# Weight sums by accumulating transfers in a seven-product feed-forward block (one core of Trainium2)

## The chip, the cores and the metric

The kernel runs on one core of one Trainium2 chip. Its time is device time in microseconds (us) of one launch; lower is better. Shown for the kernel before are three runs and one profiled execution.

## The reference

The reference is an encoder trunk of two layers on 512 positions of width 1024, in float32. Each layer is a half-step feed-forward block, a token mixer, and another feed-forward block, each with a residual and a layer norm. The change touches only the feed-forward blocks:

```python
def swiglu(x, w_gate, w_up, w_down):
    return (jax.nn.silu(x @ w_gate) * (x @ w_up)) @ w_down
```

`w_gate` and `w_up` are 1024 x 2816, `w_down` is 2816 x 1024. The block's result is halved, added to the scaled input, and normalised.

## The kernel before, in words

Every matrix product is made as three products of rounded parts: `split` (L90) makes of a float32 tile a rounded half (`hi`, tag `whi` for weights, ScalarE, L92) and a remainder (`lo`, tag `wlo`, VectorE, L94), and `mm3` (L124) issues hi*hi, hi*lo and lo*hi to the tensor engine (L127 to L129). A weight tile is fetched by SyncE's queue into a `raw` buffer (`fetch`, L104) and then split (`halves`, L112). There are four `raw` buffers and five each of `whi` and `wlo`; a buffer is taken again when its last reader is done.

Three of the four feed-forward blocks run as `ffn7` (L324), three times in the program. The 22 blocks of 128 hidden columns are made two at a time (a group) by `up` (L341), 11 groups. The first nine groups' share of the product with `w_down` is computed by a scheme with seven products in place of eight: the hidden columns of a pair, the two halves of the positions and the two halves of the output columns form a 2 x 2 by 2 x 2 block product. The activations' seven combinations are made in `up` (L378 to L381, tile `hb`, split into `sl`). After every third group, `down` (L394) does the weights' part for the three groups, nine times in the whole program. It works in two units: a long one of two groups (tiles of 128 x 1024, 512 KB) and a short one of one group (128 x 512, 256 KB). A unit's four weight blocks are w11 and w12 (own buffers `b11`, `b12`, two each, one for each unit) and w21 and w22 (`raw` buffers).

In a unit the first four products need p2, the split of w21; p1, the split of w11; q4, the split of a sum of all four blocks; and q5, the split of t1 = w11 + w12 (a `raw` buffer too). The sums are made in place, by VectorE:

```python
tt(out=t1, in0=w11, in1=w12, op=ALU.add)     # L417
tt(out=w12, in0=w12, in1=w22, op=ALU.add)    # L418
tt(out=w11, in0=w11, in1=w12, op=ALU.add)    # L419
tt(out=w21, in0=w21, in1=w11, op=ALU.add)    # L420
```

PE then takes p2, q4, p1, q5 of the long unit (12 matmuls each), p2, q4, p1, q5 of the short one (6 each), and after them the summed w11, w22 (fetched again) and the summed w12 of both units. PE's order is as written; the order of the instructions on the other engines, and of the loads on SyncE's queue, is set by a scheduler when the program is built, and each engine runs its own in that order. The next group's gate weights are fetched into the `raw` buffers that the short unit leaves. GpSimd has, in these blocks, only the small steps of the layer norm (L145, L146, L180), behind the last groups.

Of the kernel before, what the change touches and what calls it, by code (L numbers as in the profile page):

```python
# [14 lines left out]
ALU = mybir.AluOpType  # L15
# [34 lines left out]
class Trunk:  # L50
# [273 lines left out]
    def ffn7(self, xt, wg, wu, wd, g_ap, b_ap, out=None, fetch=None, groups=(3, 3, 3), res=4):  # L324
# [3 lines left out]
        nc, tc = self.nc, self.tc  # L328
        tt = nc.vector.tensor_tensor
# [4 lines left out]
        with tc.tile_pool(name="act", bufs=1, reuse_waits="tile") as ap, \  # L334
# [50 lines left out]
            def part(b, banks, js, w, start, stop, onto=False):  # L385

                hi, lo = w
                for i, j in enumerate(js):
                    for t in range(2):
                        c = slice(t * P, t * P + P)  # L390
                        self.mm3(banks[t], slots[j][:, 0, b, c], slots[j][:, 1, b, c], hi[:, i], lo[:, i],
                                 start and i == 0, stop and i == len(js) - 1, onto)

            def down(gi):  # L394

                js = list(range(first[gi], first[gi + 1]))
                units = [js[i:i + 2] for i in range(0, len(js), 2)]
                Y, Z, X, V = ([self.bank() for _ in range(2)] for _ in range(4))  # L400

                def take(banks, half, col, scale):
                    for t in range(2):
                        self.add_to(xt[2 * half + t][:, col * 512:col * 512 + 512], banks[t], scale)
                held = []
                for u in units:
                    shape, rows = [len(u), 512], slice(u[0], u[-1] + 1)
                    at_end = u is units[0], u is units[-1]
                    w11, w12 = (ap.tile([P] + shape, F32, tag=n, name=n, bufs=2) for n in ("b11", "b12"))
                    w21 = self.fetch(b21[:, rows], shape)  # L410
                    p2 = self.halves(w21, shape)
                    nc.sync.dma_start(w11, b11[:, rows])
                    p1 = self.halves(w11, shape)
                    nc.sync.dma_start(w12, b12[:, rows])
                    w22 = self.fetch(b22[:, rows], shape)
                    t1 = self.w.tile([P] + shape, F32, tag="raw", name="raw", bufs=RAW)
                    tt(out=t1, in0=w11, in1=w12, op=ALU.add)  # L417
                    tt(out=w12, in0=w12, in1=w22, op=ALU.add)  # L418
                    tt(out=w11, in0=w11, in1=w12, op=ALU.add)  # L419
                    tt(out=w21, in0=w21, in1=w11, op=ALU.add)  # L420
                    q4 = self.halves(w21, shape)
                    q5 = self.halves(t1, shape)
                    part(1, Y, u, p2, *at_end)
                    part(2, Z, u, q4, *at_end)
                    part(0, X, u, p1, *at_end)
                    part(3, V, u, q5, *at_end)
                    held.append((u, shape, rows, w11, w12))
                take(Y, 0, 0, 0.5)
                take(Z, 1, 0, 0.5)
                take(X, 0, 0, 0.5)  # L430
                take(V, 1, 1, 0.5)
                for u, shape, rows, w11, w12 in held:
                    part(4, X, u, self.halves(w11, shape), False, u is units[-1], True)
                take(X, 0, 1, -0.5)
                for u, shape, rows, w11, w12 in held:
                    part(6, V, u, self.load(b22[:, rows], shape), False, u is units[-1], True)
                take(V, 0, 1, 0.5)
                for u, shape, rows, w11, w12 in held:
                    part(5, X, u, self.halves(w12, shape), False, u is units[-1], True)
                take(X, 1, 1, -0.5)  # L440
                take(X, 1, 0, 0.5)

            with self.as_written(mybir.EngineType.PE):
                for fg in range(NF // 2):
                    up(fg)
                    if fg == 0 and fetch is not None:
                        xt = fetch()
                    if fg + 1 in first:
                        down(first.index(fg + 1) - 1)
# [19 lines left out]
            g, b = self.ln_params(g_ap, b_ap, ap)  # L469
# [939 lines left out]
```

## Time and profile before

| | |
|---|---|
| median of three runs | 1802.85 us (1802.31 to 1803.46) |
| profiled execution, its own time | 1803.46 us |
| span of the profile | 1801.7 us |
| PE, DVE, ACT, POOL busy | 1782.3, 1103.5, 709.2, 34.8 us |
| transfers | 213.57 MB, mean 119 GB/s |

Engines: PE is the tensor engine, DVE VectorE, ACT ScalarE, POOL GpSimd, SP SyncE; "q" behind a name means its instruction queue, where transfers are issued. A row of the instruction timeline gives its start and length in us, the engine, the source line, the operation, the tiles written and read, their form, and in brackets how long the engine had been idle before and what it waited for. A row of transfer issues gives the tile and its source, the number, the size of one and the median time from issue to landing.

### The profile page before, as it was taken

Reading aid. Unit: us, or ns where it says so; the run is one execution under the profiler, and the core shown is the slowest. Engines: PE = TensorE matmul, PEld = TensorE weight load, DVE = VectorE, ACT = ScalarE, POOL = GpSimd, SP = SyncE. Lnnn points to the kernel's source line nnn. Section 1 sums busy time; section 2 is a strip of 40 time slices with the busy share of each in tenths; the row PEclk is TensorE's granted clock in tenths of the full one; section 3 lists DMA queues with packets and bytes.
Section 4 is the critical chain, followed back from the end, with each engine's and each line's share of the span. In section 5 each row is a group of like instructions: output and inputs, shape, how many; then the busy total and the mean of one; then the engine's idle time right before and its main releaser. Section 6 shows DMA issues by size and latency. Waiting matters only on the chain.

```text
span 1801.7 us, 22457 instructions
## 1 busy us (share of the span) xinstructions
PE 1782.3 (99%) x8754; PEld 1494.7 (83%) x8754; DVE 1103.5 (61%) x1812; ACT 709.2 (39%) x1019; POOL 34.8 (2%) x119
## 2 busy tenths in 40 slices
PE   9999999999999999999999999999999999999998
PEld 8888888898887888888889888888888898888886
DVE  7956432276766657474746575757488566566664
ACT  4233421255776443333334333333354343333341
POOL 0000000010000100000000000000020000000000
PEclk9999999999999999999999999999999999999999
DMA  6345633255413544243243251514323251515131
GB/s 211 107 125 172 204 100 101 94 172 161 138 62 98 179 167 155 73 134 94 78 151 106 76 163 59 158 59 123 117 88 95 70 182 60 162 62 162 48 127 47
DMA packets 169338, 213.57 MB, mean 119 GB/s; under 512 B 8208, under 2 KB 128784, under 8 KB 169232
## 3 DMA queue, kind: packets, MB, share of 16 engines
q1 hardware_dynamic: 169232, 212.14, 37.5%
q8 instruction: 68, 1.11, 0.3%
q14 instruction: 38, 0.31, 0.1%
HBM read 196.91 MB, written 14.16 MB: 117 GB/s over the span
## 4 chain that ended last, share of the span: by engine, by line
issue 59%; PE 35%; DVE 3%; POOL 1%; ACT 1%; DMA 1%; POOLq 0%; DVEq 0%; ACTq 0%
PE ps L127 11%; PE ps L128 11%; PE ps L129 11%; PE ps L851 1%; POOL rs L146 1%; DVE wlo L94 0%; PE ps L901 0%; PE ps L136 0%; PE ps L893 0%; DVE pl L94 0%; POOL st L180 0%; DMA s5tl<-side 0%; POOL rs L145 0%; DMA raw<-in_wg_dram 0%; PE ps L892 0%
## 5 line engine op out<-in xcount | busy, mean ns | idle before, releaser
L127 PE MATMUL ps<-xh,whi 128*128 128x512 f32 (+1 forms) x1696 | 637.5, 376 | 1.4 <-ACT xh L92 1.4
L128 PE MATMUL ps<-xl,whi 128*128 128x512 f32 (+1 forms) x1696 | 633.3, 373 | 1.7 <-DVE xl L94 1.7
L129 PE MATMUL ps<-xh,wlo 128*128 128x512 f32 (+1 forms) x1696 | 632.9, 373 | 0.0
L94 DVE TENSOR_TENSOR wlo<-raw,whi 128x1024 fp32r<-128x1024 f32 (+1 forms) x325 | 376.0, 1162 | 396.7 <-ACT whi L92 396.1
L92 ACT ACTIVATE whi<-raw 128x1024 fp32r<-128x1024 f32 (+1 forms) x325 | 328.4, 1012 | 604.5 <-PE ps L128 383.1
L127 PEld LDWEIGHTS ps<-xh,whi 128*128 128x128 f32 x1696 | 319.4, 188 | 60.4 <-issue 3.1
L128 PEld LDWEIGHTS ps<-xl,whi 128*128 128x128 f32 x1696 | 319.5, 188 | 56.9 <-DVE xl L94 2.4
L129 PEld LDWEIGHTS ps<-xh,wlo 128*128 128x128 f32 x1696 | 319.4, 188 | 56.4
L127 PE MATMUL ps<-whi,sl 128*128 128x512 f32 x426 | 165.7, 389 | 0.0
L128 PE MATMUL ps<-wlo,sl 128*128 128x512 f32 x426 | 165.7, 389 | 0.0
L129 PE MATMUL ps<-whi,sl 128*128 128x512 f32 x426 | 165.4, 389 | 0.0
L165 DVE SCALAR_TENSOR_TENSOR xb<-ps,xb 128x512 f32<-128x512 f32 x176 | 113.9, 687 | 38.9 <-PE ps L129 38.6
L129 PEld LDWEIGHTS ps<-whi,sl 128*128 128x128 f32 x426 | 80.0, 188 | 16.7
L128 PEld LDWEIGHTS ps<-wlo,sl 128*128 128x128 f32 x426 | 80.0, 188 | 16.6
L127 PEld LDWEIGHTS ps<-whi,sl 128*128 128x128 f32 x426 | 80.0, 188 | 16.6
L368 ACT ACTIVATE th<-ps 128x512 f32<-128x512 f32 x66 | 38.8, 593 | 110.5 <-PE ps L129 110.4
L374 DVE TENSOR_TENSOR hb<-th,ps 128x512 f32<-128x512 f32 x54 | 36.7, 688 | 64.8 <-PE ps L129 64.8
L94 DVE TENSOR_TENSOR sl<-hb,sl 128x1792 fp32r<-128x1792 f32 x27 | 54.6, 2023 | 31.9 <-ACT sl L92 31.9
L92 ACT ACTIVATE whi<-b 128x1024 fp32r<-128x1024 f32 (+1 forms) x54 | 45.8, 849 | 66.9 <-PE ps L129 64.8
L92 ACT ACTIVATE sl<-hb 128x1792 fp32r<-128x1792 f32 x27 | 45.9, 1700 | 44.7 <-DVE hb L381 44.7
L94 DVE TENSOR_TENSOR wlo<-b,whi 128x1024 fp32r<-128x1024 f32 (+1 forms) x54 | 50.7, 952 | 6.1 <-ACT whi L92 6.1
L127 PE MATMUL ps<-whi,xh 128*128 128x256 f32 (+1 forms) x160 | 49.9, 312 | 0.3 <-ACT xh L92 0.3
(339 smaller groups left out, 1953.6 us busy)
## 6 DMA issues: line engine op xcount, KB each, us to landing
raw<-in_wg_dram SPq DMA_DIRECT2D x88, 512.0 KB, 4.4
raw<-in_wu_dram SPq DMA_DIRECT2D x88, 512.0 KB, 3.9
raw<-in_wd_dram SPq DMA_DIRECT2D x61, 512.0 KB, 3.3
raw<-in_ab_in_dram SPq DMA_DIRECT2D x20, 512.0 KB, 4.3
b<-in_wd_dram SPq DMA_DIRECT2D x18, 512.0 KB, 5.1
raw<-in_wd_dram SPq DMA_DIRECT2D x27, 256.0 KB, 2.6
raw<-in_cd_in_dram SPq DMA_DIRECT2D x12, 512.0 KB, 3.6
b<-in_wd_dram SPq DMA_DIRECT2D x18, 256.0 KB, 5.3
```

Of the source, the lines that this page charges most:

```text
L92: nc.scalar.activation(out=hi, in_=src, func=AF.Copy, scale=scale)
L94: nc.vector.tensor_tensor(out=lo, in0=src, in1=hi.bitcast(F32), op=ALU.subtract)
L127: mm(ps, ah, bh, start=start, stop=False)
L128: mm(ps, ah, bl, start=False, stop=False)
L129: mm(ps, al, bh, start=False, stop=stop)
L146: nc.gpsimd.tensor_tensor(out=v[:, 1:2], in0=v[:, 0:1], in1=self.cst[:, 0:1], op=ALU.pow)
L165: self.nc.vector.scalar_tensor_tensor(out=zz, in0=p, scalar=scale, in1=zz, op0=ALU.mult, op1=ALU.add, **({} if total is None else {"accum_ ...
L368: nc.scalar.activation(out=th, in_=bk[0, f], func=AF.Silu)
L374: tt(out=hb[:, 0::7] if f == 0 else hb[:, 1:3], in0=th.rearrange("p (a c) -> p a c", a=2), in1=bk[1, f].rearrange("p (a c) -> p a c", a=2) ...
L851: nc.tensor.matmul(banks[h][:, o:o + w], a[r, i * P:i * P + P], b[r, :w], start=n == 0, stop=n == 2)
```

## The change

The last three of a unit's four adds are replaced by transfers that add the source buffer to what the destination buffer holds. They are issued by GpSimd. t1 stays on VectorE.

```diff
                     tt(out=t1, in0=w11, in1=w12, op=ALU.add)
-                    tt(out=w12, in0=w12, in1=w22, op=ALU.add)
-                    tt(out=w11, in0=w11, in1=w12, op=ALU.add)
-                    tt(out=w21, in0=w21, in1=w11, op=ALU.add)
+                    for a, b in ((w12, w22), (w11, w12), (w21, w11)):
+                        nc.gpsimd.dma_start(a, b, accum_op=ALU.add)
                     q4 = self.halves(w21, shape)
                     q5 = self.halves(t1, shape)
```

PE's and SyncE's instructions keep their order. Lines behind L418 have a number that is one lower after the change. DVE around the first `down`, before; of the long unit b11_6169 is w11, raw_6171 w21, raw_6185 t1, of the short one b11_6246 is w11, b12_6247 w12, raw_6248 w21, raw_6260 w22 and raw_6262 t1:

```order
L94 TENSOR_TENSOR wlo_6179<-b11_6169,whi_6178 128x1024
L419 TENSOR_TENSOR b11_6169<-b11_6169,b12_6170 128x1024
L420 TENSOR_TENSOR raw_6171<-raw_6171,b11_6169 128x1024
L94 TENSOR_TENSOR wlo_6191<-raw_6171,whi_6190 128x1024
L417 TENSOR_TENSOR raw_6262<-b11_6246,b12_6247 128x512
L418 TENSOR_TENSOR b12_6247<-b12_6247,raw_6260 128x512
L94 TENSOR_TENSOR wlo_6195<-raw_6185,whi_6194 128x1024
L374 TENSOR_TENSOR hb_6147<-th_6148,ps_6085 128x2x256
```

The same place after the change, on to the short unit's q4 (wlo_6268) and q5 (wlo_6272):

```order
L94 TENSOR_TENSOR wlo_6179<-b11_6169,whi_6178 128x1024
L94 TENSOR_TENSOR wlo_6191<-raw_6171,whi_6190 128x1024
L94 TENSOR_TENSOR wlo_6195<-raw_6185,whi_6194 128x1024
L417 TENSOR_TENSOR raw_6262<-b11_6246,b12_6247 128x512
L374 TENSOR_TENSOR hb_6147<-th_6148,ps_6085 128x2x256
L374 TENSOR_TENSOR hb_6147<-th_6151,ps_6086 128x512
L379 TENSOR_TENSOR hb_6147<-hb_6147 128x256
L378 TENSOR_TENSOR hb_6147<-hb_6147 128x256
L94 TENSOR_TENSOR wlo_6251<-raw_6248,whi_6250 128x512
L380 TENSOR_TENSOR hb_6147<-hb_6147 128x256
L381 TENSOR_TENSOR hb_6147<-hb_6147 128x256
L94 TENSOR_TENSOR wlo_6256<-b11_6246,whi_6255 128x512
```

The adds are gone, and the short unit's t1 stands behind the remainder of the long q5, where it stood ahead of it. The remainders of q4 (wlo_6191) and, in the short unit, of p1 (wlo_6256) keep their places in the row.

GpSimd after the change, from the last layer-norm step ahead of the first `ffn7` to the second `down`'s first transfers (b12_6170 is w12 and raw_6183 w22 of the long unit):

```order
L146 TENSOR_TENSOR rs_5608<-rs_5608,cst_63 128x1
L419 DMA b12_6170<-raw_6183 128x1024
L419 DMA b11_6169<-b12_6170 128x1024
L419 DMA raw_6171<-b11_6169 128x1024
L419 DMA b12_6247<-raw_6260 128x512
L419 DMA b11_6246<-b12_6247 128x512
L419 DMA raw_6248<-b11_6246 128x512
L419 DMA b12_6820<-raw_6833 128x1024
```

Before, the next layer-norm step of GpSimd (L180) followed here; now 18 transfers of a block stand ahead of it, six for each `down`.

## Rows read from the trace of the kernel before

**Rows 1.** The page: busy time by engine, and one costly group of PE.
```profile
PE 1782.3 (99%) x8754; PEld 1494.7 (83%) x8754; DVE 1103.5 (61%) x1812; ACT 709.2 (39%) x1019; POOL 34.8 (2%) x119
...
L128 PE MATMUL ps<-xl,whi 128*128 128x512 f32 (+1 forms) x1696 | 633.3, 373 | 1.7 <-DVE xl L94 1.7
```

**Rows 2.** Busy us by stretch: length, PE, PEld, DVE, ACT, POOL, clock, DMA share, GB/s.
```profile
648.50:684.50 36.00, 36.00 (x161) 29.80 (x160) 19.88 (x21) 10.17 (x12) 0.00 (x0) 1.00 0.19 61
684.50:713.20 28.70, 28.70 (x128) 23.79 (x127) 24.75 (x35) 13.47 (x15) 0.00 (x0) 1.00 0.46 142
...
872.10:900.80 28.70, 28.70 (x128) 23.76 (x127) 24.76 (x35) 13.48 (x15) 0.00 (x0) 1.00 0.33 94
```

**Rows 3.** Two of the adds by line: ns min/median/max, first and last start, forms.
```profile
L418 DVE TENSOR_TENSOR b<-b,raw x18: 692/959/1227, 655.5 to 1691.8; 128x1024 f32<-128x1024 f32 x9, 128x512 f32<-128x512 f32 x9
...
L420 DVE TENSOR_TENSOR raw<-raw,b x18: 691/960/1227, 672.5 to 1704.5; 128x1024 f32<-128x1024 f32 x9, 128x512 f32<-128x512 f32 x9
```

**Rows 4.** Timeline of DVE around the first `down`.
```profile
669.95 1.22 DVE L94 TENSOR_TENSOR wlo<-b,whi 128x1024 fp32r<-128x1024 f32 x1
...
674.88 1.22 DVE L94 TENSOR_TENSOR wlo<-raw,whi 128x1024 fp32r<-128x1024 f32 x1 [1.19 <-ACT whi L92]
676.14 0.69 DVE L417 TENSOR_TENSOR raw<-b,b 128x512 f32<-128x512 f32 x1
...
683.97 1.37 DVE L374 TENSOR_TENSOR hb<-th,ps 128x512 f32<-128x512 f32 x2 [2.67 <-PE ps L129]
...
688.08 0.69 DVE L94 TENSOR_TENSOR wlo<-b,whi 128x512 fp32r<-128x512 f32 x1 [0.68 <-ACT whi L92]
...
689.53 0.69 DVE L420 TENSOR_TENSOR raw<-raw,b 128x512 f32<-128x512 f32 x1
```

**Rows 5.** Timeline of ACT around the first `down`.
```profile
673.79 1.06 ACT L92 ACTIVATE whi<-raw 128x1024 fp32r<-128x1024 f32 x1
...
687.96 1.69 ACT L92 ACTIVATE sl<-hb 128x1792 fp32r<-128x1792 f32 x1
690.35 0.63 ACT L92 ACTIVATE whi<-raw 128x512 fp32r<-128x512 f32 x1 [0.70 <-DVE raw L420]
...
705.05 1.06 ACT L92 ACTIVATE whi<-raw 128x1024 fp32r<-128x1024 f32 x1 [0.72 <-PE ps L129]
```

**Rows 6.** Timeline of PE in the first `down`.
```profile
687.40 0.39 PE L128 MATMUL ps<-wlo,sl 128*128 128x512 f32 x1
...
695.56 0.39 PE L128 MATMUL ps<-wlo,sl 128*128 128x512 f32 x1
...
696.92 0.39 PE L128 MATMUL ps<-wlo,sl 128*128 128x512 f32 x1
```

**Rows 7.** Transfer issues: count, size of one, median us to landing.
```profile
raw<-in_wg_dram SPq DMA_DIRECT2D x88, 512.0 KB, 4.4
...
raw<-in_wd_dram SPq DMA_DIRECT2D x61, 512.0 KB, 3.3
...
raw<-in_wd_dram SPq DMA_DIRECT2D x27, 256.0 KB, 2.6
...
x<-in_x_dram SPq DMA_DIRECT2D x6, 512.0 KB, 6.8
...
x<-in_x_dram SPq DMA_DIRECT2D x4, 256.0 KB, 5.5
...
side<-side SPq DMA_DIRECT2D x32, 32.0 KB, 2.0
```

**Rows 8.** Timeline of SP's queue around the first `down`.
```profile
677.59 4.07 SPq L106 DMA_DIRECT2D raw<-in_wd_dram  x2
692.79 1.78 SPq L106 DMA_DIRECT2D raw<-in_wg_dram  x2
```

**Rows 9.** GpSimd: a group by line, and its first step behind the first `ffn7`'s `down`s.
```profile
L145 POOL TENSOR_SCALAR rs<-mv 128x1 f32<-128x1 f32 x4 | 3.7, 928 | 22.2 <-DVE mv L1234 17.0 <-DVE pm L1264 5.2
...
952.65 0.19 POOL L180 TENSOR_TENSOR st<-st 128x1 f32<-128x1 f32 x1 [330.77 <-ACT ps L176]
```

## The prediction

> **What bounds the kernel now.** I read the page first, then busy time by stretches, then the order of events around one of the changed adds. The page's busy times [rows 1] have the tensor engine (PE) at 1782.3 of 1801.7 us, so whatever is not PE's own work costs time only where it makes PE wait. The stretches [rows 2] show this at the changed place: in the last 36 us before a `down` and in the 28.7 us of the `down` itself PE is busy 36.00 of 36.00 and 28.70 of 28.70 us, at a granted clock of 1.00 (its 2.4 GHz level). DVE has 16 us free in the first stretch and 4 in the second. All nine `down`s read alike (the first and, of the third, the `down` itself are shown), so what one costs is taken nine times.
>
> Next, when PE needs what. In the first `down`, which PE begins at about 684.5 with the long unit's p2, the first product with the long q4's remainder starts at 687.40, the one with the short p2's remainder at 695.56, with the short q4's at 696.92 [rows 6]; each rounded half is wanted 0.23 us sooner. ACT takes the summed long w21 at 673.79 [rows 5]; the sum of the short one ends on DVE at 689.53 + 0.69 = 690.22 [rows 4]. So the long q4 has 13.6 us from its sum to PE, the short one 6.7, of which the split itself takes some. **The short unit is the tight place.**
>
> **What is removed.** Three adds in each of 18 units, 54 in all, at medians of 959 and 960 ns for two of them [rows 3] and the third like them: 54 x 0.96 = 51.8 us of DVE. It is worth nothing: PE does not wait for DVE here [rows 2]. In the whole run PE's idle time is 1801.7 - 1782.3 = 19.4 us, and none of it lies in these stretches.
>
> **What is added.** 54 transfers on chip, 27 of 512 KB and 27 of 256 KB, each waiting for the one before. Call L the time of a long one from the end of its wait to landing, S that of a short one. The first (w12 += w22) has no bearing in the long unit: its inputs are ready when the pair sum t1 is (DVE starts the first add that it replaces at 655.5 [rows 3]), 15 us before the second is allowed.
>
> The second (w11 += w12) overwrites w11, so it waits for the remainder of p1, which DVE ends at 669.95 + 1.22 = 671.17 [rows 4]. The third lands at 671.17 + 2L. ACT then rounds (1.06 us [rows 5]) and DVE subtracts (1.22 us): with 0.1 us of hand-over the long q4 is ready at 673.5 + 2L. PE asks for it at 687.40: **no stall in the long unit up to L = 6.9 us**.
>
> But DVE and ACT work in order, and the late q4 holds up what stands behind it. DVE can begin q4's remainder at 671.17 + 2L + 1.13 = 672.30 + 2L. Behind it come q5's remainder, t1 of the short unit, the five steps of the third activation group and two short remainders, the last of them p1's: 1.26 + 1.26 + 0.73 + 4.12 = 7.37 us by the starts and lengths in [rows 4] (674.88 to 676.14 for a long remainder; 0.69 and 0.04 to the next for the short t1; 683.97 to 688.77 less 0.68 us of idle time for the rest). So the short p1 remainder ends at 679.67 + 2L if that is later than now, 688.08 + 0.69 = 688.77: up to L = 4.55 nothing moves. Call this time E. The first short transfer starts after the short t1, at 675.55 + 2L, and lands S later; if that is later than E, it takes E's place.
>
> From E the second and third short transfers take 2S, then ACT 0.63 and DVE 0.69 us with 0.15 of hand-over [rows 4, 5]. PE asks at 696.92. **Stall per `down` = E + 2S - 695.44.** With E as now, S may be 3.33 us; with L above 4.55 the stall is 2(L + S) - 15.77, so L + S may be 7.9 us.
>
> **The price of L and S.** No transfer in the profile is issued by GpSimd, none accumulates, and the only ones between buffers on chip are of 32 KB, 2.0 us [rows 7]. From below: plain loads of the same weights, landing after 3.3 us (512 KB) and 2.6 us (256 KB), medians. From above: the slowest plain loads of these sizes, x's, at 6.8 and 5.5 us [rows 7]. An accumulating transfer must read both operands. The two plain medians give 0.7 us for 256 KB over 1.9 us that do not depend on size; charging the bytes twice gives 1.9 + 2.8 = 4.7 and 1.9 + 1.4 = 3.3 us. GpSimd's issue comes on top: its one-column operations take 0.19 to 0.93 us [rows 9], and I take the upper end, 0.9, since making a transfer's list is more work than one column. So **L = 5.6, S = 4.2**, nearer to the plain loads because the transfer queues are quiet here (share 0.19 and 0.46 in [rows 2]). The upper bounds get the second reading too: 6.8 + 1.4 = 8.2 and 5.5 + 0.7 = 6.2.
>
> The Trainium skill, "DMA: Bandwidth & Descriptors", section "Rules for kernel authors", says that an accumulating transfer reads its destination and writes it later; no run here shows it yet. With that alone and no price for the issue, 4.7 and 3.3, an estimate, the stall would be 2 x 8.0 - 15.77 = 0.2 us per `down`, some 2 us in all.
>
> **The sum.** E: 679.67 + 11.2 = 690.87, against 675.55 + 11.2 + 4.2 = 690.95 for the first short transfer; the later counts. Stall 690.95 + 8.4 - 695.44 = 3.9 us, nine times 35 us. Against the profiled execution's own 1803.46 us that is 1838.7; the median of the three runs stands 0.6 lower, so **1838 us**, 2.0% slower.
>
> **What else moves, at no price.** SP's order of loads is the same, but its waits are not. The short b22 load, second of the pair begun at 677.59, now waits for the first short transfer, some 9 us later; behind it the next group's gate weights, issued at 692.79 [rows 8], wait for the short q4 split, to about 701. They land after 4.4 us [rows 7], at 705; ACT wants the first at 705.05 now [rows 5] and 3.9 us later then, and PE not before the `down` ends at 713.2. If that cover goes, the next group starts late by the shortfall. The third activation group reaches PE's short unit (remainder needed at 695.56 [rows 6]) through DVE and ACT behind the late q4: 672.30 + 2L + 6.7 for its last step, 1.69 for its rounding [rows 5] and 1.22 x 1.75 = 2.1 for its remainder of 1792 columns by the 1024 of [rows 4], so 694.0 at L = 5.6; it becomes a stall of its own from L = 6.4. On GpSimd the 18 transfers of a feed-forward block stand ahead of its layer-norm steps; the first of these runs at 952.65 [rows 9], 52 us after the last `down` of that block ends at about 901, so it is covered.
>
> **Rivals.**
> *Hidden.* An accumulating transfer costs what a plain load of its size does: L + S = 3.3 + 2.6 = 5.9, under 7.9, and S under 3.33. No stall, 1803 us, not slower. For it: the slack is real and the queues are quiet. Against it: the bytes are read twice, and a software engine issues. It decides as long as L + S stays under 7.9 and S under 3.33. Chance 0.18. The Trainium skill, same page, section "Anatomy of one DMA — SWDGE (gpsimd) path", speaks for this one: it fits a GpSimd transfer as 2.0 us plus its bytes at 436 GB/s, an estimate of 3.2 and 2.6 us, so no stall and 1803 us. The plain loads of [rows 7] agree with it, but SP issued those.
>
> *Dear.* The transfers are slow themselves: L = 8.2, S = 6.2. Then E = 675.55 + 16.4 + 6.2 = 698.15, the stall 698.15 + 12.4 - 695.44 = 15.1, nine times 136 us, 1939 us. For it: three transfers in series multiply any error, each us on both L and S costs 4 to 5 us per `down`. Against it: the quiet queues. Chance 0.28 for anything over 1880.
>
> *Not as written.* That the adds stay on DVE somewhere is excluded by the order: 54 DVE rows are gone, 54 GpSimd rows are there. That DVE's relief shortens something: the only idle time of PE behind DVE among the page's groups is 1.7 us [rows 1], under the 0.2% (3.6 us) that a measurement can tell from no change; 0.02 for a gain that I do not see.
>
> **How the numbers follow.** My forecast, a stall of 0.4 to 8.5 us per `down`, 1807 to 1880 us, has 0.52; with the dear case slower has 0.80; the hidden case gives same 0.18, the rest faster 0.02. The range runs from the hidden case, 1802, to the dear one, 1940. Costs beyond that end I give about 0.1. Within the forecast's own case the range is 1807 to 1880.
>
> **What would show it.** Right: PE idle some 4 us once in each `down`, at its short q4 (12 us into it), behind DVE's remainder or ACT's rounding of w21; GpSimd transfers landing after about 5.6 and 4.2 us; PE's stretch of 28.7 us becoming about 32.6; 18 adds left on DVE in the `down`s out of 72. Wrong: no idle time of PE in the `down`s (hidden); a first stall at the long q4, 2.7 us in (L above 6.9); stalls that differ from one `down` to the next (contention instead of a fixed price); or idle time at the start of the next group (the late gate weights).

## The result and the profile after

The change is slower: 1826.93 us (median of four runs, 1824.29 to 1830.34) against 1802.58 for the kernel before (four runs), a ratio of 1.0137 with a 95% interval of 1.0125 to 1.0148. The profiled execution took 1824.29 us, its span is 1822.6.

The page's busy times show the exchange: DVE is relieved of 56 us, GpSimd and a transfer queue of its own have them, and PE, whose work is the same, is done 21 us later. Answers to [rows 1]:

```profile
PE 1788.6 (98%) x8754; PEld 1492.6 (82%) x8754; DVE 1047.4 (57%) x1758; ACT 705.7 (39%) x1019; POOL 81.0 (4%) x173
...
q0 software_dynamic: 7776, 21.24, 6.1%
```

The stretches around the first `down` and behind it (the columns of [rows 2]) say where: PE is still busy for the whole 36 us before the `down`; in the `down` it is busy 29.57 of 31.60 us, and in the 28.8 us behind it again all the time.

```profile
646.60:682.60 36.00, 36.00 (x161) 29.80 (x160) 14.58 (x16) 10.15 (x12) 2.78 (x3) 1.00 0.35 83
682.60:714.20 31.60, 29.57 (x128) 23.64 (x127) 23.96 (x35) 13.15 (x15) 2.59 (x3) 1.00 0.62 181
714.20:743.00 28.80, 28.80 (x129) 23.84 (x128) 13.74 (x17) 9.05 (x9) 0.00 (x0) 1.00 0.50 149
```

From its first product to the end of its last the first `down` lasts 31.59 us, where it lasted 28.72; all nine last 30.86 to 31.78, together 22.4 us more. So the whole loss lies in the `down`s (the rest of this execution is 1.5 us shorter than in the one before, by the two spans). The list of PE's waits (total, times, longest) has three rows that were not there before, nine times each:

```profile
PE ps L127 <- ACT whi L92: 6.7, 9, 1.3
PE ps L127 <- DVE xb L165: 6.0, 9, 0.7
...
PE ps L128 <- DVE wlo L94: 2.0, 9, 0.2
```

The timeline of PE in the first `down` puts them in place:

```profile
694.56 0.39 PE L129 MATMUL ps<-whi,sl 128*128 128x512 f32 x1
696.10 0.51 PE L127 MATMUL ps<-whi,sl 128*128 128x512 f32 x1 [1.15 <-ACT whi L92]
696.82 0.51 PE L128 MATMUL ps<-wlo,sl 128*128 128x512 f32 x1 [0.22 <-DVE wlo L94]
...
701.64 0.47 PE L127 MATMUL ps<-whi,sl 128*128 128x512 f32 x1 [0.66 <-DVE xb L165]
```

The first pair of waits is at the short q4, where the prediction had it: PE comes to it 12.2 us into the `down` and waits for its rounded half, then for its remainder. The third row is the start of the next part, the summed w11 onto the banks X: PE waits until DVE has emptied them (`take`, L165). The list shows less than the waits cost. Products that follow each other start every 0.23 us, but the list counts a wait only from the end of the product ahead, 0.39 us or more behind its start. By the starts the first `down` loses 696.10 - 694.56 - 0.23 = 1.31 us ahead of the product with q4's rounded half, 0.49 more ahead of the one with its remainder and 0.82 at X; and behind the second and the third of these products the next one starts after 0.34 and 0.31 us in place of 0.23. So the three waits, 14.7 us in the list, are 22.4 us in the `down`s.

GpSimd's timeline of the first `down` shows the chain that leads there, six transfers in the order of the program:

```profile
654.15 1.05 POOL L419 DMA_DIRECT2D b<-raw  x1 [34.18 <-DVE raw L417]
669.58 0.87 POOL L419 DMA_DIRECT2D b<-b  x1 [14.38 <-DVE wlo L94]
674.32 0.86 POOL L419 DMA_DIRECT2D raw<-b  x1 [3.87 <-DMA b<-b]
683.33 0.86 POOL L419 DMA_DIRECT2D b<-raw  x1 [8.16 <-DVE raw L417]
687.93 0.86 POOL L419 DMA_DIRECT2D b<-b  x1 [3.74 <-issue]
692.09 0.87 POOL L419 DMA_DIRECT2D raw<-b  x1 [3.30 <-DMA b<-b]
```

and ACT's and DVE's timelines what becomes of the landings (ACT rounds both q4s as soon as their transfers land; DVE, idle for 10.57 and 6.22 us before q4's remainders, does what is queued behind them late):

```profile
678.75 2.01 ACT L92 ACTIVATE whi<-raw 128x1024 fp32r<-128x1024 f32 x2 [6.22 <-DMA raw<-b]
...
695.41 1.15 ACT L92 ACTIVATE whi<-raw 128x512 fp32r<-128x512 f32 x2 [7.62 <-DMA raw<-b]
```

```profile
679.84 2.36 DVE L94 TENSOR_TENSOR wlo<-raw,whi 128x1024 fp32r<-128x1024 f32 x2 [10.57 <-ACT whi L92]
682.12 0.68 DVE L417 TENSOR_TENSOR raw<-b,b 128x512 f32<-128x512 f32 x1
...
696.08 1.29 DVE L94 TENSOR_TENSOR wlo<-raw,whi 128x512 fp32r<-128x512 f32 x2 [6.22 <-ACT whi L92]
697.29 0.68 DVE L165 SCALAR_TENSOR_TENSOR xb<-ps,xb 128x512 f32<-128x512 f32 x1
...
699.02 4.27 DVE L165 SCALAR_TENSOR_TENSOR xb<-ps,xb 128x512 f32<-128x512 f32 x7
```

The price of a transfer, from issue to landing, by size (answers to [rows 7]; all three of a long unit have the same median):

```profile
b<-raw POOLq DMA_DIRECT2D x9, 512.0 KB, 4.4
...
b<-raw POOLq DMA_DIRECT2D x9, 256.0 KB, 3.9
b<-b POOLq DMA_DIRECT2D x9, 256.0 KB, 3.6
raw<-b POOLq DMA_DIRECT2D x9, 256.0 KB, 3.2
```

The three short ones differ. The first two run beside loads of w22 for the products behind (SyncE issues the second of these at 687.43, when the first transfer has left its buffer), the third runs alone:

```profile
687.43 0.33 SPq L106 DMA_DIRECT2D raw<-in_wd_dram  x1
```

### The profile page after: what moved, and what is told of

Same layout as the page of the kernel before. It is cut to its first block, busy times and chain, and to the rows that moved or that the text cites. A ratio compares the mean times of both kernels' runs of the same rounds, so it can differ in the third digit from the quotient of the medians.

```text
span 1822.6 us, 22576 instructions
## 1 busy us (share of the span) xinstructions
PE 1788.6 (98%) x8754; PEld 1492.6 (82%) x8754; DVE 1047.4 (57%) x1758; ACT 705.7 (39%) x1019; POOL 81.0 (4%) x173
## 4 chain that ended last, share of the span: by engine, by line
PE 37%; DMA 11%; issue 8%; DVE 4%; ACT 1%; POOLq 0%; POOL 0%; DVEq 0%; ACTq 0%; SPq 0%
PE ps L127 12%; PE ps L129 12%; PE ps L128 12%; DMA b<-raw 4%; DMA raw<-b 4%; DMA b<-b 3%; DVE wlo L94 2%; DVE xb L165 1%; ACT whi L92 1%; DVE raw L417 1%; PE ps L136 0%; DMA lgb<-in_sgu_ln_dram 0%; ACT ps L176 0%; POOLq L419 0%; DVE zf L188 0%
## 5 line engine op out<-in xcount | busy, mean ns | idle before, releaser
L165 DVE SCALAR_TENSOR_TENSOR xb<-ps,xb 128x512 f32<-128x512 f32 x176 | 113.6, 683 | 19.8 <-PE ps L129 19.6
L129 PEld LDWEIGHTS ps<-whi,sl 128*128 128x128 f32 x426 | 80.0, 188 | 16.5
```

The lines of the kernel that those rows point to most:

```text
L129: mm(ps, al, bh, start=False, stop=stop)
L165: self.nc.vector.scalar_tensor_tensor(out=zz, in0=p, scalar=scale, in1=zz, op0=ALU.mult, op1=ALU.add, **({} if total is None else {"accum_ ...
```

## The experiments

The theory after this reading: the loss is PE's wait in the short unit, made by transfers in series that start late, and by DVE's work queued behind the late sums. The first rival: the bytes that the transfers move (21.2 MB) and GpSimd's work slow other things, wherever they stand. Two more concern the second wait and the price of a step.

| kernel | median us (runs) | ratio to before, 95% | longer `down`s, nine together, us |
|---|---|---|---|
| the change | 1826.93 (4) | 1.0137 [1.0125, 1.0148] | 22.4 |
| long units only | 1802.81 (10) | 1.0001 [0.9991, 1.001] | 0.0 |
| short units only | 1818.96 (4) | 1.0093 [1.0078, 1.0108] | 16.0 |
| same transfers, nobody waits | 1806.12 (10) | 1.0021 [1.0011, 1.0031] | 0.1 |
| first sum on VectorE | 1820.87 (4) | 1.0104 [1.0089, 1.0119] | 18.3 |
| banks X emptied sooner | 1825.68 (4) | 1.0122 [1.0105, 1.0139] | 21.6 |
| no wait for p1 | 1804.64 (10) | 1.001 [1.0001, 1.0019] | 0.9 |
| plain copies | 1807.43 (1) | one run | 1.5 |
| adds by GpSimd | 1802.98 (10) | 1.0002 [0.9992, 1.0011] | 0.0 |
| plain copies beside, two engines | 1805.65 (1) | one run | 0.0 |

The last column is from each profile: first product to end of last, less 28.72, summed.

### Long units only

```diff
-                        nc.gpsimd.dma_start(a, b, accum_op=ALU.add)
+                        if len(u) == 2:
+                            nc.gpsimd.dma_start(a, b, accum_op=ALU.add)
+                        else:
+                            tt(out=a, in0=a, in1=b, op=ALU.add)
```

> The long units' three sums by accumulating transfers, the short units' by VectorE. Chain theory (the time goes into PE's wait in the short unit, for transfers in series that start late): with 4.85 us for each long step the short p1 remainder moves from 4.3 to about 5 us into a down, two adds of 0.7 us and the split follow, q4 is ready at 8 to 9 us and PE asks at 12.2: no wait at the short q4, the second wait (the banks that DVE empties late) under 0.3 us; 1802 to 1806 us. Traffic theory (the added 21.2 MB slow the loads or the engines): two thirds of the bytes are still moved, so two thirds of the loss stay, about 1819 us.

1802.81 us: two thirds of the bytes are still moved, and nothing is lost. The stretch of the first `down` (columns of [rows 2]) has PE busy throughout, with a DMA share of 0.53 against 0.46 before:

```profile
683.50:712.20 28.70, 28.70 (x128) 23.77 (x127) 25.90 (x37) 13.58 (x15) 0.00 (x0) 1.00 0.53 166
```

The traffic theory's 1819 is out. The long unit's chain by itself is fully covered.

### Short units only

```diff
+                        if len(u) == 1:
```

(with the same two branches).

> The short units' three sums by accumulating transfers, the long units' by VectorE. Chain theory: the first short transfer is no longer late, since t1 of the short unit comes early again, so the second starts at 4.4 us into the down (5.1 in the change), two steps of 3.8 and 3.4 us and the split follow: q4's remainder ready at about 13.0, PE asks at 12.47: a wait of 0.3 to 1.2 us, and the second wait stays at about 0.5 to 0.8; 1809 to 1818 us. Traffic theory: a third of the bytes, a third of the loss, about 1811 us, with the loss not at these two places of PE.

1818.96 us, a little over the range. A third of the bytes makes two thirds of the loss. PE's waits are at the same three places; in six of nine `down`s the wait for the rounded half is gone and that for the remainder and for X stay, here the third `down`:

```profile
888.82 0.50 PE L128 MATMUL ps<-wlo,sl 128*128 128x512 f32 x1 [0.15 <-DVE wlo L94]
893.64 0.47 PE L127 MATMUL ps<-whi,sl 128*128 128x512 f32 x1 [0.67 <-DVE xb L165]
```

The wait for X stays at 0.63 to 0.69 us, as expected. The long units' part of the loss, 22.4 - 16.0 = 6.4 us, appears only together with the short units' transfers: late long sums delay the short t1 (L417 0.4 us ahead of the first `down` in the change, 8.3 ahead in [rows 4]), and with it the first short transfer and the load of w22 that waits for it. The second short transfer then starts on average 5.1 us into the `down` in place of 4.6 and takes 0.2 us longer to land.

The other three `down`s (the first, the fourth and the last) lose 0.8 to 1.7 us more than these six. There the second short transfer lands after 4.0 to 4.8 us in place of 3.2, and beside it the trace has one packet of 16 KB of a queue named instruction (q8), which the six do not have there. The transfers in the 5 us around it, in the last `down` and, below the dots, in the third:

```profile
q8 instruction: 1, 0.02, 1.9%
b<-b POOLq DMA_DIRECT2D x1, 256.0 KB, 4.8
...
b<-b POOLq DMA_DIRECT2D x1, 256.0 KB, 3.2
```

The packet falls 5 to 6 us into the same three `down`s in the kernel before as well, where nobody waits for a transfer. That it is the cause is read from the coincidence alone.

### The same transfers, and nobody waits for them

To the kernel before, whose sums stay on VectorE, this adds (the lines that make and clear the two buffers are left out; the sources are w12, w11 and w21, in the change w22, w12 and w11):

```diff
+                    for a, b in zip(scr, (w12, w11)):
+                        nc.gpsimd.dma_start(a[:, 0:len(u)], b, accum_op=ALU.add)
+                    nc.gpsimd.dma_start(scr[0][:, 0:len(u)], w21, accum_op=ALU.add)
```

> The kernel before, all sums on VectorE, and beside them the same 54 accumulating transfers of the same sizes from the same buffers, issued by GpSimd, but into two buffers of their own that nobody reads (cleared by GpSimd at the start of each block). Chain theory: nobody waits for them but the loads that take their source buffers again, 4 to 8 us later; PE idle in the downs under 0.3 us each; 1802 to 1806 us. Traffic theory: the same bytes and the same issue work, so the same loss, about 1825 us; a share of it if only part comes from traffic.

PE is busy throughout the first `down` again, at a higher DMA share (0.64) than in the change (0.62):

```profile
684.30:713.00 28.70, 28.70 (x128) 23.79 (x127) 24.75 (x35) 13.46 (x15) 1.76 (x2) 1.00 0.64 180
```

The time is 1806.12, at the upper end of what the chain theory expected. The 3.5 us over the kernel before lie outside the `down`s, 2.7 of them between the end of the sixth `down` and the start of the seventh, where the second token mixer runs: this execution takes 261.8 us there in place of 259.1. One place makes the difference: PE waits for VectorE once for 2.07 us, where it is 1.04 in the kernel before, and in the two stretches of 4 us behind it the granted clock is 0.69 and 0.88 (columns of [rows 2]), where it was 1.00.

```profile
1335.12 0.50 PE L129 MATMUL ps<-whi,xl 128*128 128x512 f32 x1 [2.07 <-DVE xl L94]
1335.00:1339.00 4.00, 3.88 (x12) 3.09 (x13) 3.96 (x8) 1.10 (x3) 0.00 (x0) 0.69 0.00 0
```

ScalarE's timelines show where the wait comes from: ahead of this place a step of the mixer (`vt`, L524 before) stands behind a scaling (`xb`, L193) in this build and ahead of it in the kernel before. Little is transferred meanwhile (a DMA share of 0.15 in the 4 us up to the wait's end, 0.26 there in the kernel before). So the 2.7 us go with an order of instructions that the scheduler chose in this build; the kernel with copies by two engines, below, has the same order there and the same 261.8 us. What matters here holds: the bytes, the issues and the queue cost the `down`s nothing.

### First sum on VectorE

```diff
-                    for a, b in ((w12, w22), (w11, w12), (w21, w11)):
+                    tt(out=w12, in0=w12, in1=w22, op=ALU.add)
+                    for a, b in ((w11, w12), (w21, w11)):
```

> The change, but the first of the three sums (w12 += w22) on VectorE, the other two by transfers. Chain theory: in the change the second short transfer starts at 4.84 to 5.38 us into the down, held by the landing of the first short one; here it starts when the short p1 remainder ends, at 4.3 to 5.0 us if DVE is no later, so the wait at the short q4 (1.2 to 2.1 us in the change) shrinks by 0.1 to 0.9 us per down: 1818 to 1825 us. If the late t1, not the first transfer, sets the start, no gain: 1825 to 1829 us. Traffic theory: two thirds of the loss, 1819 us, spread over everything.

1820.87, 6.1 us under the change and inside the theory's range. The list has 2.5 us (seven waits) for the rounded q4, where it had 6.7; the wait for X stays, and that for q4's remainder too, at 2.0 us:

```profile
PE ps L127 <- DVE xb L165: 5.9, 9, 0.7
PE ps L127 <- ACT whi L92: 2.5, 7, 0.5
```

But the theory's reason is not what the trace shows. The second short transfer starts no sooner, at 5.0 to 5.4 us into the `down`s where it was 4.8 to 5.4: VectorE now makes the first sum ahead of p1's remainder, and this ends about as late as the first transfer landed. In the first `down`, which begins at 683.89:

```profile
689.26 0.86 POOL L420 DMA_DIRECT2D b<-b  x1 [12.56 <-DVE wlo L94]
```

What is gained is its landing, 3.2 us after its issue in place of 3.7 on average. With the sum on VectorE, w22's buffer is free earlier, SyncE issues both loads of w22 by 685.5, and none runs beside the transfer. Nine times 0.53 us is 4.8 of the 6.1; the `down`s together are 4.1 us shorter. In the change itself the trace names the first transfer's landing as what releases the second in seven of nine `down`s; this run does not show that taking that wait away wins anything. By the total alone the traffic theory's 1819 would fit as well; it had fallen with the long units only and with the transfers that nobody waits for.

### Banks X emptied sooner

```diff
+                take(X, 0, 0, 0.5)
                 take(Y, 0, 0, 0.5)
                 take(Z, 1, 0, 0.5)
-                take(X, 0, 0, 0.5)
                 take(V, 1, 1, 0.5)
```

(The scheduler then puts X's two evacuations behind Z's and ahead of Y's.)

> The change, with the four evacuations behind a down's first products written in another order, so that VectorE empties the banks X, into which the summed w11 goes next, ahead of Y's. Theory of two waits (0.8 to 0.9 us of PE's wait per down is for X's evacuation, which stands in DVE's queue behind the late remainders): that wait falls to under 0.2 us, nine times 0.7 is 6 us, and the wait at the short q4 stays at 1.2 to 2.1 us: 1818 to 1822 us. Rival (one wait only; the later one is time that PE would lose anyway to ACT's late split of w11): no change, 1825 to 1829 us.

1825.68, no gain that these runs can tell from the change. The wait for X is gone, as the theory had it, but another has come, here in the third `down`: at the short part of the summed w11, PE now waits for its remainder, which DVE makes behind all eight evacuations.

```profile
901.18 0.50 PE L128 MATMUL ps<-wlo,sl 128*128 128x512 f32 x1 [0.24 <-DVE wlo L94]
```

By the starts of the products this costs some 0.5 us per `down`, in place of some 0.9. What that leaves of a gain went into this execution's longer waits at the short q4 (8.1 us in the list against 6.7) and into a lower clock in its second `down`, told below. My reading that the second wait comes from DVE's queue is right; that changing its order wins 6 us is wrong, since what is moved back becomes late in its turn.

### No wait for p1

q4 is w21 + w11 + w12 + w22, and t1 holds the sum of two of them already, so it can be had without touching w11:

```diff
-                    for a, b in ((w12, w22), (w11, w12), (w21, w11)):
+                    for a, b in ((w12, w22), (w21, t1), (w21, w22), (w11, w12)):
```

> Four accumulating transfers in a unit in place of three, in an order that needs no split of p1: w12 += w22, w21 += t1, w21 += w22, and w11 += w12 beside them. q4 then hangs on the split of p2 and two transfers, and not on the p1 remainder and the first transfer. Chain theory: in the short unit the p2 remainder ends about 2.2 us into the down, where the p1 remainder ended at 4.3; two steps of 3.8 us and the split later q4 is ready at 11.0 to 11.6 and PE asks at 12.47: no wait there, at most 0.4 us of the second one: 1802 to 1807 us, in spite of a third more transfers. Traffic or a dear GpSimd queue: slower than the change, 1830 us or more.

1804.64: a third more transfers, and 22 of 24 us are back. GpSimd's timeline shows the short unit's part: the first of the two transfers into w21 starts behind p2's remainder, at 687.36, 2.2 us ahead of the one that waits for p1's (689.52), and the second, at 690.82, lands in time.

```profile
687.36 0.87 POOL L419 DMA_DIRECT2D raw<-raw  x1 [6.96 <-DVE wlo L94]
689.52 0.87 POOL L419 DMA_DIRECT2D b<-b  x1 [1.29 <-DVE wlo L94]
690.82 0.87 POOL L419 DMA_DIRECT2D raw<-raw  x1 [0.42 <-DMA raw<-raw]
```

Six of the nine `down`s are back at 28.72 us; the other three are again the first, the fourth and the last, the ones with the packet of q8 beside the short transfers.

### Plain copies

```diff
-                        nc.gpsimd.dma_start(a, b, accum_op=ALU.add)
+                        nc.gpsimd.dma_start(a, b)
```

This leaves the three sums out (each transfer overwrites its destination).

> The change with plain copies in place of accumulating transfers: w22 over w12, w12 over w11, w11 over w21, so the three sums are left out. Same queue, waits and sizes; only the reading of the destination goes. Step by step in the price of my prediction: the second reading is 1.4 us of a long and 0.7 us of a short transfer, so landing after about 3.0 and 2.5 us in place of 4.4 and 3.2, the wait at the short q4 under 0.3 us, 1803 to 1810 us. Rival (the issue and a fixed latency are the price, the adding is free): landing within 0.2 us of the change's, time 1822 us or more.

The landings, and the time of 1807.43 in one run, go with the price by bytes read (the last copy of each unit, which runs alone):

```profile
raw<-b POOLq DMA_DIRECT2D x9, 512.0 KB, 2.8
...
raw<-b POOLq DMA_DIRECT2D x9, 256.0 KB, 2.2
```

Adding to the destination costs 4.4 - 2.8 = 1.6 us for 512 KB and 3.2 - 2.2 = 1.0 us for 256 KB.

### Plain copies beside, by two engines

To the kernel before, in each unit:

```diff
+                    for e, a, b in ((nc.gpsimd, "sa", w12), (nc.sync, "sb", w11)):
+                        e.dma_start(ap.tile([P] + shape, F32, tag=a, name=a), b)
```

> The kernel before, all sums on VectorE, with two plain on-chip copies more in each unit, into buffers of their own that nobody reads: w12 by GpSimd, w11 by SyncE. To part the price of a step: with the step's landing after 4.4 (512 KB) and 3.2 us (256 KB) when accumulating, and 2.8 and 2.2 when GpSimd only copies, SyncE's copies show what the issuing engine adds. If a software issue costs about 0.9 us more, SyncE's land after about 2.0 and 1.4; if the issue is not dearer, after 2.8 and 2.2 again. Nobody waits for the copies but the loads behind SyncE's in its queue: 1802 to 1810 us.

SyncE's copies land after 2.9 and 2.2 us, as GpSimd's did in the run before this: issuing from GpSimd adds nothing to a landing that can be told here, from one run of each. (GpSimd's own copies in this run land after 3.9 and 4.3 us. They run at another time, and that loads beside them are the reason is not shown.)

```profile
sb<-b SPq DMA_DIRECT2D x9, 512.0 KB, 2.9
...
sb<-b SPq DMA_DIRECT2D x9, 256.0 KB, 2.2
```

### Adds by GpSimd

```diff
-                        nc.gpsimd.dma_start(a, b, accum_op=ALU.add)
+                        nc.gpsimd.tensor_tensor(out=a, in0=a, in1=b, op=ALU.add)
```

> The three sums as adds computed by GpSimd itself, in place of transfers. Chain theory: what counts is the length of a step; if GpSimd adds 512 columns in under 3 us, and 1024 in under 4.5, q4 is ready in time, no wait in the downs: 1802 to 1806 us. Rival (whatever stands off VectorE costs, through the ports that GpSimd and VectorE share or by GpSimd's slowness): steps over 3.3 us, or DVE's instructions in the downs longer by more than 10%, and a wait again: 1815 us or more.

1802.98, the time of the kernel before, with the same 54 adds off VectorE. GpSimd's timeline of the first `down` gives the steps:

```profile
671.33 2.40 POOL L419 TENSOR_TENSOR b<-b,b 128x1024 f32<-128x1024 f32 x1 [13.33 <-DVE wlo L94]
673.81 2.38 POOL L419 TENSOR_TENSOR raw<-raw,b 128x1024 f32<-128x1024 f32 x1
...
688.94 1.29 POOL L419 TENSOR_TENSOR b<-b,b 128x512 f32<-128x512 f32 x1 [8.24 <-issue]
690.30 2.96 POOL L419 TENSOR_TENSOR raw<-raw,b 128x512 f32<-128x512 f32 x1
```

A long add of GpSimd's takes some twice as long as VectorE's (2.40 against 1.23 us) and about half as long as the transfer's step. The second short one runs beside VectorE's remainder of the activations, and both are longer than alone: 2.96 us where the first takes 1.29, and 2.40 where the remainder took 2.02 in the kernel before. This is one of the signs that the rival named, a VectorE instruction longer by more than 10%; the wait that it forecast did not come.

```profile
689.71 2.40 DVE L94 TENSOR_TENSOR sl<-hb,sl 128x1792 fp32r<-128x1792 f32 x1 [0.90 <-ACT sl L92]
```

No version was faster than the kernel before: PE has no wait in these stretches to give back.

## Why the prediction was right, and where it was off

*What bounds, and what the relief is worth.* Right. PE's busy stretches decide; three kernels that take adds from VectorE without making q4 late (long units only, no wait for p1, adds by GpSimd) stay within 0.1% of the kernel before.

*The place.* Right. The short unit's q4 is where PE waits first, ACT's rounding and DVE's remainder of it the two releasers, in all nine `down`s. That the first short transfer, held by the late t1, would set the start of the second was a close call in the working (690.95 against 690.87); in the trace it does so in eight of nine `down`s by the times (seven by the releaser named), at 5.4 us into the first where the p1 remainder has ended at 4.3. The run with that sum on VectorE did not test it, since p1's remainder then ends about as late.

*The long unit.* Right: no wait, L being under 6.9.

*The price of L and S.* L was too high, and this is the term that was mis-sized. The two long steps of the first `down` take from the end of p1's remainder, 668.05 + 1.22 = 669.27, to ACT's start at 678.75, so 4.74 us each and not 5.6. S came out nearly right, and this was luck. From the end of its wait to landing the three short steps take on average over nine `down`s 4.3, 4.3 and 3.5 us, 4.0 together, and 4.2 was taken. But the parts are others. The issue, taken as 0.9 us, is not there in the landings: GpSimd and SyncE land alike, and 0.3 to 0.5 us pass instead between the end of a wait's cause and the issue (669.27 to 669.58). The plain transfer was taken as 3.3 and 2.6 (on chip it is 2.8 and 2.2), the second reading as 1.4 and 0.7 (1.6 and 1.0). A short step that runs alone takes 3.5 us; the other 0.8 us of the first two comes with w22's loads beside them. The working had moved the second of these loads, rightly, and priced that at nothing. The measured steps in the working's place of 2L and 3S give 2.1 us for the first `down`, and by the starts q4's remainder is 1.8 late: the chain is right, its sizes were not. One reading is wrong without an effect on the time: x's loads are not the slowest of 256 KB, three others take 6.6 to 6.9 us, so that the upper bound of S should have been higher.

The Trainium skill, "DMA: Bandwidth & Descriptors", section "Rules for kernel authors", has the accumulating transfer read its destination before it writes; the landings agree, by 1.6 and 1.0 us over the plain copies. The Trainium skill's fit, same page, section "Anatomy of one DMA — SWDGE (gpsimd) path", gives an estimate of 3.2 and 2.6 us; it lies over the plain copies' 2.8 and 2.2 and under the accumulating ones' 4.4 and 3.2: it does not price the adding, and the time that followed from it, no stall, is refuted.

*The stall.* Predicted: one, of 3.9 us per `down`. Measured: at the short q4 13.7 us over nine, 1.5 each, and a second one at the banks X of some 0.9 each, which the working did not have. It had followed DVE's queue only up to the short p1 remainder, and not what stands behind q4's: q5's remainder, an evacuation, w11's long remainder and three more evacuations before X's. In the kernel before DVE is done with the first bank of X at 699.75 + 0.68 = 700.43, 0.34 us before PE comes to it:

```profile
699.75 0.68 DVE L165 SCALAR_TENSOR_TENSOR xb<-ps,xb 128x512 f32<-128x512 f32 x1
700.77 0.39 PE L127 MATMUL ps<-whi,sl 128*128 128x512 f32 x1
```

In the change DVE has all this work still before it when q4's remainder is done at 696.8, and is done with that bank at 701.5, 4.7 us later; PE's products up to X take 4.0 us from there. The difference is the wait at X, and so it is there in every `down`, at 0.63 to 0.69 us in the list, however long the wait at q4.

The two errors, a step too dear and a wait overlooked, partly cancel each other: 35 us predicted, 22.4 in the `down`s, 24 in the medians. One sign named for being wrong did show in part, stalls that differ from `down` to `down` by contention: the wait at the short q4 is 0.41 to 1.30 us in the list, and landings of one and the same short transfer differ by what runs beside them.

*Rivals.* "Hidden" fell with the three new waits. "Dear" fell with the landings of 4.4 and 3.2 us.

*What else moves, at no price.* Mostly right. The next group's gate weights are issued 14.2 us into the first `down`, where it was 8.3 ([rows 8]); 16.5 had been worked out, and PE has no wait in the 28.80 us behind the `down`. The layer-norm steps run at 958.57, far behind the transfers. What should have had a price is the moved load of w22, as told above.

```profile
696.80 0.98 SPq L106 DMA_DIRECT2D raw<-in_wg_dram  x2
```

*What stays open.* The median of the runs rose 2 us more than the nine `down`s of the profiled one. The four runs stand in the order of their mean granted clock (0.998 for 1824.29 us, 0.997 for 1826.52, 0.996 for 1827.35, 0.995 for 1830.34), so I take the rest for clock; only the first of them has a profile, so it is argued and not shown.

## What to carry to other kernels

Moving work off an engine that nobody waits for is worth nothing, and can cost as much as the new place is slower in series: count the chain from the last input to the consumer's clock time, in the smallest unit, where the slack is smallest and a fixed latency weighs most. When something comes late on an engine that works in order, follow its queue behind the late instruction to the end of the stage, not only to the first consumer. If sums must leave VectorE, look first for an order that does not wait for a buffer to be read out, then for the engine with the shortest step: here GpSimd's own add, at 2.4 us, beat the transfer's 4.7. And ask of every load that the new steps hold up what it will run beside when it comes.

## What the runs showed of the hardware that was not expected

The list of waits shows less than PE loses: 14.7 us against 22.4, and by the starts of the products most of the difference is the way in which a wait is counted. What a restart adds by itself is 0.1 us in these rows, a gap of 0.34 or 0.31 us to the next product in place of 0.23.

A wait can also be followed by a lower clock. In the second `down` of the run with X emptied sooner, PE waited 1.75 and 0.22 us at the short q4, the longest wait seen in a `down`, and then had a granted clock of 0.68 and 0.90 in the next two stretches of 4 us (columns of [rows 2]); the single products there, 0.63 us long in place of 0.39, are those of the lower level, 1.2 GHz:

```profile
796.00:800.00 4.00, 3.71 (x10) 2.73 (x11) 3.71 (x5) 3.06 (x5) 0.00 (x0) 0.68 0.48 137
800.00:804.00 4.00, 4.00 (x18) 3.22 (x17) 3.48 (x6) 1.70 (x2) 0.00 (x0) 0.90 0.69 257
```

By these rows 4 x 0.32 + 4 x 0.10 = 1.7 us were lost, and that `down` was the longest of all, 32.89 us. The wait of 2.07 us in the mixer, above, was followed by the same: 4 x 0.31 + 4 x 0.12 = 1.7 us, and with the 1.0 us by which the wait itself was longer this is the 2.7 found there. It does not follow every wait of this length: in the run with the short units only PE waits 1.77 us in the mixer, and the clock stays at 1.00. The change's own first `down`, with 1.15 and 0.22 us of waiting, kept a clock of 1.00 too.

From GpSimd, accumulating transfers of 512 KB land after 4.4 us, copies after 2.8, and the issue takes 0.87 us of GpSimd each. One of 256 KB that runs alone lands after 3.2 us; beside loads it took 3.5 to 4.2 in the change, and 4.6 once, with the packet of q8 as well.
